# Loading the small state-space matrices of a hybrid decoder layer: C as four 128-row blocks, B with its states on the partitions

## The chip, the cores and the metric

The kernel runs on one core of one Trainium2 chip. The metric is the time of one execution on the device in microseconds; the runs of a kernel are summed up by their median. One execution was also recorded by the hardware profiler, and every time of an instruction below comes from that record. Its engines are PE (matrix multiply, with PEld for its weight loads), DVE (vector), ACT (activation), POOL and SP. Here SP does nothing but issue DMA transfers.

## The reference, cut to what matters

A layer on a sequence of 1,024 positions with 1,024 features: RMS norm, one input projection, two mixers (a diagonal complex state-space mixer and a short gated convolution), a gate for each, one output projection, a residual and a last norm. The change concerns the parameters of the state-space mixer, whose 32 groups have 16 channels (h) and 64 complex states (p) each:

```python
u32 = u.astype(f32).reshape(bsz, seq, SSM_N_GROUPS, SSM_GROUP)       # 32 groups x 16
q_re = (p_re * a_re + p_im * a_im) / den
q_im = (p_im * a_re - p_re * a_im) / den
bb_re = q_re[..., None] * b_re - q_im[..., None] * b_im              # b: (32 g, 64 p, 16 h)
bb_im = q_re[..., None] * b_im + q_im[..., None] * b_re
bu_re = jnp.einsum('blgh,gph->blgp', u32, bb_re)
bu_im = jnp.einsum('blgh,gph->blgp', u32, bb_im)
...
_, _, s_re, s_im = lax.associative_scan(
    _scan_combine, (a_seq_re, a_seq_im, bu_re, bu_im), axis=1)
y = (jnp.einsum('blgp,ghp->blgh', s_re, c_re.astype(f32))            # c: (32 g, 16 h, 64 p)
     - jnp.einsum('blgp,ghp->blgh', s_im, c_im.astype(f32))
     + d_skip.astype(f32) * u32)
```

In DRAM, c lies with p innermost (64 floats, 256 bytes in a row) and b with h innermost (16 floats, 64 bytes in a row).

## The kernel before

**Staging.** Products are float32 split into a high and a low part, so each is three matrix products ("h", "l", "x": weights high times input high, weights low times input high, weights high times input low). The input is 128 positions to a tile, eight tiles x0 to x7; they are normed on DVE, turned by PE transposes (`turn`), and written by ACT as xh (`gain`, L218) and by DVE as the low rest xl (`rest`, L224). The first projection computes u for four blocks of 128 channels (uw0 to uw3) and two halves of the positions. Then come the convolution's projections (`conv_hc`, `conv_bz`), among which the state-space mixer's steps for four blocks of eight groups are laid, then the gates and the output projection.

**The order at the start is written by hand.** The string START (L33 to L35) is run through token by token under a manual schedule for PE, ACT and DVE; each engine keeps this order. A letter names a step and digits its tiles: s = square of an x tile on ACT, n = norm on DVE, t = transposes of a pair of x tiles on PE, g = `gain` of that pair on ACT, x = `rest` on DVE, u/U = matrix products of u, k = `keep_u`, p = `transpose_params`, C = turned copies of C (L433 to L435), d = the next steps of `discretise` on DVE. The stretch that matters reads `k00 p0 u11lx. k10 t2 u21lx. k20 u31lx. k30 d12 g2 s6 x2 s7 C n67`. Behind the manual part a scheduler merges the rest of the program into each engine's order, by its own estimates.

**keep_u** (L241) copies a finished half block of u from PSUM to the SBUF tile `us` on ACT (L243), and SP stores it to the DRAM scratch `uscr` in four transfers of 64 KB (L245). The tile has two buffers, so the third copy (k20) needs the first's four stores to have landed, and the fourth (k30) the second's.

**The transfers** of all inputs are issued by SP in program order: x0, weights, x1 to x3, the small parameters, x4 to x7, and behind these the two loads of C into `craw` (32 groups on the partitions) and three loads of B into the rows 32 to 63 of `cb` (b_re, b_im, b_re), each of 32 rows of 4 KB. Completion of SP's transfers is told by eight semaphores used in turn; each transfer waits for the one eight places earlier.

**From C and B to c1, c2, b1, b2.** These four tiles [128, 32 groups, 16 h] hold the states of the real part on partitions 0 to 63 and of the imaginary part on 64 to 127 (c1 is (re, -im), c2 is (-im, -re), b1 is (re, im), b2 is (-im, re)). ACT first copies C with its axes turned into rows 0 to 31 of `cb`, three times (re, im, re; L435). `transpose_params(1)` and `(2)` (L270 to L277) then transpose, for each h, the 64 rows (32 groups of C, 32 of B) with 128 columns: 16 transposes each, 32 in all, in PSUM tiles of eight; ACT evicts each tile in two pieces, one to b and one to c, with the sign as a scale. b1 and b2 are read by the six `discretise` steps that make bb and bs (L396 to L401); c1 and c2 and these by `ssm_prep` (rr, vv; L499 to L505), whose result `vv` goes into the matrix products `ps_k` (L544).

Of the kernel before, what the change touches and what calls it, by code (L numbers as in the profile page):

```python
# [10 lines left out]
F32 = mybir.dt.float32  # L11
F32R = mybir.dt.float32r
I32 = mybir.dt.int32
AF = mybir.ActivationFunctionType
# [5 lines left out]
P = 128  # L20
# [3 lines left out]
C = L // T  # L24
KT = D // P
NB = 4
G = 8
NG = 32
H = 16
S = 64  # L30
EPS = 1e-6
WARM = (26, 8, 14)
START = ("s0 w0 n0 c s1 W0 n1 W1 w1 t0 L0 g0 L1 U010hl x0 u010x. W2 s2 s3 W3 L2 n23 u20hx u30hx t1 L3 g1 u230l. s4 x1 s5 n45 "  # L33
         "U01231h u01lx. k00 p0 u11lx. k10 t2 u21lx. k20 u31lx. k30 d12 g2 s6 x2 s7 C n67 d12 U01232h u01232l t3 g3 d8 x3 u01232x. "
         "U01233h u03l p1 p2 u03x. k01 u13lx. k11 d u23lx. k21 u33lx. k31")  # L35
ORDER = "p0 0 1 2 m0 q0 i0 3 p1 4 o0 5 6 m1 q1 i1 7 p2 8 o1 9 m2 q2 i2 10 p3 11 o2 m3 q3 i3 12 13 o3 14 15"
MAGIC = 12582912.0
# [20 lines left out]
def hybrid_kernel(ctx: ExitStack, tc, x, norm_gain, w_in, a_re, a_im, log_dt, b_re, b_im,  # L58
                  c_re, c_im, d_skip, w_glu, b_glu, conv_w, w_out, final_gain, out):
    nc = tc.nc  # L60
    V, A, Q, PE = nc.vector, nc.scalar, nc.gpsimd, nc.tensor

    const = ctx.enter_context(tc.tile_pool(name="const", bufs=1))
    big = ctx.enter_context(tc.tile_pool(name="big", bufs=1))
# [3 lines left out]
    psm = ctx.enter_context(tc.tile_pool(name="psm", bufs=4, space=PSUM))  # L68
# [6 lines left out]
    ident = const.tile([P, P], F32, name="ident")  # L75
    make_identity(nc, ident)
    sgn = const.tile([P, 1], F32, name="sgn")
    V.memset(sgn[0:S], 1.0)
    V.memset(sgn[S:P], -1.0)
    nsgn = const.tile([P, 1], F32, name="nsgn")  # L80
# [44 lines left out]
    pst = tc.alloc_tile_pool(name="pstage", bufs=1, side="right")  # L125
# [1 line left out]
    par = tc.alloc_tile_pool(name="par", bufs=1)  # L127
    xpool = tc.alloc_tile_pool(name="xstage", bufs=8)

    cb = big.tile([2 * NG, 3 * S * H], F32, tag="cy", name="cb")  # L130
    cb = cb.rearrange("g (r p h) -> g r p h", h=H, r=3)
    craw = pst.tile([NG, 2, H, S], F32, name="craw")
    lam_r = pst.tile([NG, 2, 2, S], F32, name="lam_r")
    ldt = pst.tile([P, NG], F32, name="ldt")
    d_r = pst.tile([NG, H], F32, name="d_r")
# [17 lines left out]
    def load(seq):  # L153
        for i in seq:
            if i == "w":
                n = len(raw)
                wr = (wst.tile([P, KT, P], F32, tag="wr", name=f"wru{n}", bufs=2) if n < 2 else
                      ysb[:, 1 if n == 2 else 3].rearrange("p (k n) -> p k n", k=KT))
                nc.sync.dma_start(wr, w_in_k[:, :, n * P:n * P + P])
                raw.append(wr)  # L160
            else:
                load_x(i)
# [7 lines left out]
    nc.sync.dma_start(rows, conv_w[0].rearrange("k (b p) -> (k b) p", p=P))  # L170
    nc.sync.dma_start(rowb, b_glu[0].rearrange("(b p) -> b p", p=P))
    load((4, 5, 6, 7))
    nc.sync.dma_start(craw[:, 0], c_re[0])
    nc.sync.dma_start(craw[:, 1], c_im[0])
    for k, src in enumerate((b_re, b_im, b_re)):
        nc.sync.dma_start(cb[NG:2 * NG, k], src[0])


    pw = pmm.tile([P, P], F32, tag="mm", name="ps_warm")
    def warm(count):  # L180
        for n in range(count):
            PE.transpose(pw, ident, ident)
# [4 lines left out]
    def square(i):  # L187
        ss = const.tile([P, 2], F32, tag="ss", name=f"ss{i}", bufs=4)
        sq = ysb[:, 2]
        sums[i] = []  # L190
        for k, c in enumerate(halves(i)):
            A.activation(sq[:, c], x_t[i][:, c], AF.Square, accum_out=ss[:, k:k + 1])
            sums[i].append(ss[:, k:k + 1])

    def norm(*tiles):
        todo = [rsqrt_steps(sums[i]) for i in tiles]
        for ops in itertools.zip_longest(*[ops for ops, _ in todo]):
            for op in filter(None, ops):
                op()
        for i, (_, r) in zip(tiles, todo):  # L200
            cut = D // 2 if i < 4 else D
            for c in range(0, D, cut):
                V.tensor_scalar_mul(x_t[i][:, c:c + cut], x_t[i][:, c:c + cut], r)
# [10 lines left out]
    def gain(pair, pss):  # L214
        n = slice(pair % 2 * 256, pair % 2 * 256 + 256)
        for kt in range(KT):
            ps = pss[kt // 2][:, kt % 2].rearrange("p a b -> p (a b)")
            A.activation(xh[pair // 2][:, kt, n], ps, AF.Copy, scale=g1[:, kt:kt + 1])  # L218
# [30 lines left out]
    lam = par.tile([P, 2, NG], F32, name="lam")  # L249
    c1 = par.tile([P, NG, H], F32, name="c1")  # L250
    c2 = par.tile([P, NG, H], F32, name="c2")
    b1 = pst.tile([P, NG, H], F32, name="b1")
    b2 = pst.tile([P, NG, H], F32, name="b2")
    dT = par.tile([H, NG], F32, name="dT")

    def transpose_params(part):
        if part == 0:
            ps = psm.tile([P, 2, NG], F32, tag="sm", name="ps_lam")
            for k in range(2):
                PE.transpose(ps[:, k], lam_r[:, k].rearrange("g d p -> g (d p)"), ident[0:NG, 0:NG])  # L260
            A.copy(lam, ps)
            ps = psm.tile([P, 16 + NG], F32, tag="sm", name="ps_rows")
            PE.transpose(ps[:, 0:12], rows, ident[0:12, 0:12])
            PE.transpose(ps[:, 12:16], rowb, ident[0:NB, 0:NB])
            PE.transpose(ps[0:H, 16:16 + NG], d_r, ident[0:NG, 0:NG])
            A.copy(cw, ps[:, 0:12])
            A.copy(bg, ps[:, 12:16])
            A.copy(dT, ps[0:H, 16:16 + NG])
            return
        off = part - 1  # L270
        for q in range(2):
            hs = slice(q * 8, q * 8 + 8)
            ps = psm.tile([P, 8, 2 * NG], F32, tag="sm", name=f"ps_cb{off}{q}")
            for h in range(8):
                PE.transpose(ps[:, h], cb[:, off:off + 2, :, 8 * q + h].rearrange("g r p -> g (r p)"), ident[0:2 * NG, 0:2 * NG])
            for dst, lo, scale in ((b2 if off else b1, NG, nsgn if off else 1.0), (c2 if off else c1, 0, -1.0 if off else sgn)):
                A.activation(dst[:, :, hs], ps[:, :, lo:lo + NG].rearrange("p h g -> p g h"), AF.Copy, scale=scale)  # L277

# [5 lines left out]
    def discretise(count=None):  # L286
        for op, args, kw in steps[:count]:
            op(*args, **kw)
        del steps[:count]
# [134 lines left out]
    with tc.manual_schedule(engines={mybir.EngineType.PE, mybir.EngineType.Activation, mybir.EngineType.DVE}):  # L424
        for what in START.split():
            n = [int(v) for v in what[1:] if v.isdigit()]
            if what[0] == "s":
                square(n[0])
            elif what[0] == "w":
                warm(WARM[n[0]])  # L430
            elif what[0] == "d":
                discretise(int(what[1:]) if what[1:] else None)
            elif what[0] == "C":  # L433
                for k in range(3):
                    A.copy(cb[0:NG, k], craw[:, k % 2].rearrange("g h p -> g p h"))  # L435
            elif what[0] == "c":
                ps = pmm.tile([P, KT], F32, tag="mm", name="ps_g1")
                PE.transpose(ps, g1r, ident[0:KT, 0:KT])
                V.tensor_copy(g1, ps)
            elif what[0] == "W":  # L440
                uw[n[0]] = [wst.tile([P, KT, P], F32R, tag=m, name=f"{m}u{n[0]}", bufs=4) for m in ("wh", "wl")]
                A.copy(uw[n[0]][0], raw[n[0]])
            elif what[0] == "L":
                V.tensor_tensor(uw[n[0]][1], raw[n[0]], uw[n[0]][0].bitcast(F32), SUB)
            elif what[0] == "n":
                norm(*n)
            elif what[0] == "t":
                turned[n[0]] = turn(n[0])
            elif what[0] == "g":
                gain(n[0], turned[n[0]])  # L450
            elif what[0] == "x":
                rest(n[0], turned[n[0]])
            elif what[0] == "p":
                transpose_params(n[0])
            elif what[0] in "uU":
                blocks, quarter = n[:-1], n[-1]
                cols = slice(quarter % 2 * 256, quarter % 2 * 256 + 256)
                parts = what.strip("uU0123.")
                for b in blocks:
                    if quarter % 2 == 0 and "h" in parts:  # L460
                        ups[b] = pmm.tile([P, 512], F32, tag="mm", name=f"mm_u{b}{quarter // 2}")
                if what[0] == "u":
                    todo = [(b, part, range(KT)) for b in blocks for part in parts]
                else:
                    todo = [(b, part, [kt - lag]) for kt in range(KT + 4) for lag, part in zip((0, 4), parts)
                            if 0 <= kt - lag < KT for b in blocks]
                for b, part, kts in todo:
                    product(uw[b], quarter // 2, ups[b], part, cols, what[-1] == "." and part == parts[-1], kts)
            else:
                keep_u(n[0], n[1], ups[n[0]])  # L470
# [7 lines left out]
    cy = big.tile([P, NB, L], F32, tag="cy", name="cy")  # L478
# [368 lines left out]
    for j in pairs:  # L847
# [32 lines left out]
        steps, r = rsqrt_steps([part[:, 2:3], part[:, 3:4], part[:, 4:5]])  # L880
# [44 lines left out]
```

## Time and profile before

| what | us |
|---|---|
| median of 3 runs | 437.37 |
| lowest and highest of them | 437.13, 706.63 |
| the profiled execution | 435.54 |
| its span, first to last instruction | 433.7 |
| PE busy in the span | 418.2 |
| DVE busy | 331.2 |
| ACT busy | 181.6 |

The profile's rows give the start and the duration in us, the engine, the line of the program, the operation, output and inputs by their names (numbers of buffers left out), the shape and the count of instructions merged into the row; in brackets stands how long the engine had been idle before it, and which instruction ended that. Rows of narrow stretches of time give busy shares of PE, PEld, DVE, ACT and POOL, the granted clock of PE, the busy share of the 16 DMA engines, and GB/s. DMA rows of a stretch count packets, which are the contiguous pieces of a transfer (with a few 4-byte ones that report completion).

### The profile page before, as it was taken

To read this page: it belongs to the slowest core of one execution; us is meant where nothing else is said; L and a number is where in the kernel's file an instruction comes from. 1 tells how busy PE (TensorE), PEld (TensorE's weight loads), DVE (VectorE), ACT (ScalarE), POOL (GpSimd) and SP (SyncE) were. 2 spreads that over 40 slices of the span, in tenths; PEclk is the share of its full clock that TensorE was granted. 3 is DMA by queue.
4 is the path that set the end of the run, shared out by engine and by line. 5 is a ranking of instruction groups with operands and counts; after the bars stand their busy time and mean duration, and the time that the engine had idled before them with its cause. 6 is when DMAs were issued, how large, how long until landed. Compare 5 with 4: busy or idle time off the path is not lost. (4 is left out here: it accounts for less than half of the span.)

```text
span 433.7 us, 6302 instructions
## 1 busy us (share of the span) xinstructions
PE 418.2 (96%) x2226; PEld 358.1 (83%) x2226; DVE 331.2 (76%) x821; ACT 181.6 (42%) x322; POOL 32.0 (7%) x39
## 2 busy tenths in 40 slices
PE   8998999999997999999999999999999999999991
PEld 8898999888887888888888888888888888888881
DVE  4973888969989979986996928746456799977734
ACT  4754933074213245135324414647434654333121
POOL 0000003001020020100021000211202100000011
PEclk9999999999999999999999999999999999999997
DMA  7983005433260641254025422577534540333212
GB/s 240 251 256 80 19 2 158 134 91 105 54 166 3 175 116 47 77 147 146 6 47 147 117 81 75 180 200 237 122 109 74 143 123 2 117 125 103 92 48 99
DMA packets 49472, 48.97 MB, mean 113 GB/s; under 512 B 6696, under 2 KB 39488, under 8 KB 49440
## 3 DMA queue, kind: packets, MB, share of 16 engines
q1 hardware_dynamic: 47568, 45.16, 35.5%
q0 software_dynamic: 1728, 3.15, 4.2%
q8 instruction: 17, 0.28, 0.3%
q10 hardware_dynamic: 144, 0.26, 0.2%
q14 instruction: 15, 0.12, 0.1%
HBM read 31.65 MB, written 8.39 MB: 92 GB/s over the span
## 5 line engine op out<-in xcount | busy, mean ns | idle before, releaser
L826 ACT ACTIVATE sq<-xr 128x512 f32<-128x512 f32 (+1 forms) x17 | 10.3, 606 | 41.8 <-DVE xr L823 30.1
L641 POOL TENSOR_TENSOR cy<-cy,sg 128x512 f32<-128x512 f32 x8 | 13.8, 1725 | 187.8 <-DVE sg L640 154.9
L747 PE MATMUL glu<-shl,wg 128*128 128x512 f32 x96 | 21.9, 389 | 0.0
L747 PEld LDWEIGHTS glu<-shl,wg 128*128 128x128 f32 x96 | 18.0, 188 | 3.7
L224 DVE SCALAR_TENSOR_TENSOR xl<-ps_x,g,xh 128x256 fp32r<-128x256 f32 x32 | 12.9, 474 | 8.6 <-ACT xh L218 8.6
L230 PE MATMUL mm_u<-xh,whu 128*128 128x256 f32 x128 | 17.5, 288 | 1.7 <-ACT xh L218 1.7
L230 PEld LDWEIGHTS mm_u<-xh,whu 128*128 128x128 f32 x128 | 16.2, 191 | 2.4 <-ACT xh L218 2.1
L230 PE MATMUL mm_u<-xh,wlu 128*128 128x256 f32 x128 | 17.9, 285 | 0.0
L230 PE MATMUL mm_u<-xl,whu 128*128 128x256 f32 x128 | 17.5, 284 | 0.0
L819 PE MATMUL ow<-bs,ax 128*128 128x512 f32 (+1 forms) x54 | 16.9, 367 | 0.5 <-DVE xr L823 0.5
L230 PE MATMUL mm_h<-xh,wlh 128*128 128x512 f32 x64 | 16.5, 394 | 0.0
L230 PE MATMUL mm_b<-xh,whb 128*128 128x512 f32 x64 | 16.5, 397 | 0.0
L230 PEld LDWEIGHTS mm_u<-xh,wlu 128*128 128x128 f32 x128 | 16.3, 191 | 0.1
L230 PEld LDWEIGHTS mm_u<-xl,whu 128*128 128x128 f32 x128 | 16.2, 192 | 0.1
L230 PE MATMUL mm_h<-xh,whh 128*128 128x512 f32 x64 | 16.1, 391 | 0.0
L230 PE MATMUL mm_b<-xl,whb 128*128 128x512 f32 x64 | 15.9, 390 | 0.0
L230 PE MATMUL mm_h<-xl,whh 128*128 128x512 f32 x64 | 15.8, 389 | 0.0
L230 PE MATMUL mm_c<-xh,whc 128*128 128x512 f32 x64 | 15.8, 389 | 0.0
L230 PE MATMUL mm_z<-xh,wlz 128*128 128x512 f32 x64 | 15.8, 389 | 0.0
L230 PE MATMUL mm_c<-xl,whc 128*128 128x512 f32 x64 | 15.8, 389 | 0.0
L230 PE MATMUL mm_z<-xl,whz 128*128 128x512 f32 x64 | 15.8, 389 | 0.0
L230 PE MATMUL mm_zs<-xh,wlzs 128*128 128x512 f32 x64 | 15.8, 389 | 0.0
(351 smaller groups left out, 1108.3 us busy)
## 6 DMA issues: line engine op xcount, KB each, us to landing
ee<-ec SPq DMA_DIRECT2D x16, 256.0 KB
wro<-in_w_out_dram SPq DMA_DIRECT2D x8, 512.0 KB
xr<-in_x_dram SPq DMA_DIRECT2D x8, 512.0 KB
out_dram<-xr SPq DMA_DIRECT2D x7, 512.0 KB
x<-in_x_dram SPq DMA_DIRECT2D x6, 512.0 KB
wrh<-in_w_in_dram SPq DMA_DIRECT2D x4, 512.0 KB
wrc<-in_w_in_dram SPq DMA_DIRECT2D x4, 512.0 KB
uscr<-us SPq DMA_DIRECT2D x32, 64.0 KB
```

The lines of the kernel that those rows point to most:

```text
L224: V.scalar_tensor_tensor(xl[pair // 2][:, kt, n], ps, g1[:, kt:kt + 1], hs.bitcast(F32), MUL, SUB)
L230: PE.matmul(ps[:, n], a[:, kt], b[half][:, kt, n], start=what == "h" and kt == 0, stop=last and kt == KT - 1)
L641: Q.tensor_tensor(yb[:, n], yb[:, n], sg, MUL)
L747: PE.matmul(ps, wg[:, a, k, es], shl[half][:, y, k], start=m + k == 0, stop=m == 2 and k == NB - 1)
L819: PE.matmul(out_, aq[op_a, j][:, p, k], bq[op_b, k][:, q, cols], start=first and m + k == 0, stop=m == 2 and k == NB - 1, skip_group_check ...
L826: A.activation(temp(f"sq{final_square.n}")[:, 0:x.shape[-1]], x, AF.Square, accum_out=acc)
```

## The change

C is loaded with 128 rows (8 groups by 16 h) on the partitions, for four blocks, with re, im and re beside one another (`craw`, [128, 4, 3, 64]). One transpose of 128x128 then gives one block of c1 (re, im) or of c2 (im, re), so that there are 2 x 4 transposes, each set of four in one PSUM tile and with one eviction. B is not transposed: SP loads b1 and b2 straight into their places, states on the partitions, by four transfers of 64 partitions x 32 groups x 16 floats, that is in pieces of 64 bytes at a distance of 4 KB in DRAM. b2's sign is set by one ACT operation in place. The token C goes, and the tile `cb` with it.

```diff
-         "U01231h u01lx. k00 p0 u11lx. k10 t2 u21lx. k20 u31lx. k30 d12 g2 s6 x2 s7 C n67 d12 U01232h u01232l t3 g3 d8 x3 u01232x. "
+         "U01231h u01lx. k00 p0 u11lx. k10 t2 u21lx. k20 u31lx. k30 d12 g2 s6 x2 s7 n67 d12 U01232h u01232l t3 g3 d8 x3 u01232x. "
...
-    cb = big.tile([2 * NG, 3 * S * H], F32, tag="cy", name="cb")
-    cb = cb.rearrange("g (r p h) -> g r p h", h=H, r=3)
-    craw = pst.tile([NG, 2, H, S], F32, name="craw")
+    craw = pst.tile([P, NB, 3, S], F32, name="craw")
...
-    nc.sync.dma_start(craw[:, 0], c_re[0])
-    nc.sync.dma_start(craw[:, 1], c_im[0])
-    for k, src in enumerate((b_re, b_im, b_re)):
-        nc.sync.dma_start(cb[NG:2 * NG, k], src[0])
+    for k, src in enumerate((c_re, c_im, c_re)):
+        nc.sync.dma_start(craw[:, :, k], src[0].rearrange("(b g) h p -> (g h) b p", g=G))
+    b1 = pst.tile([P, NG, H], F32, name="b1")
+    b2 = pst.tile([P, NG, H], F32, name="b2")
+    for dst, srcs in ((b1, (b_re, b_im)), (b2, (b_im, b_re))):
+        for k, src in enumerate(srcs):
+            nc.sync.dma_start(dst[k * S:k * S + S], src[0].rearrange("g p h -> p g h"))
...
-        for q in range(2):
-            hs = slice(q * 8, q * 8 + 8)
-            ps = psm.tile([P, 8, 2 * NG], F32, tag="sm", name=f"ps_cb{off}{q}")
-            for h in range(8):
-                PE.transpose(ps[:, h], cb[:, off:off + 2, :, 8 * q + h].rearrange("g r p -> g (r p)"), ident[0:2 * NG, 0:2 * NG])
-            for dst, lo, scale in ((b2 if off else b1, NG, nsgn if off else 1.0), (c2 if off else c1, 0, -1.0 if off else sgn)):
-                A.activation(dst[:, :, hs], ps[:, :, lo:lo + NG].rearrange("p h g -> p g h"), AF.Copy, scale=scale)
+        ps = psm.tile([P, NB, P], F32, tag="sm", name=f"ps_c{off}")
+        for b in range(NB):
+            PE.transpose(ps[:, b], craw[:, b, off:off + 2].rearrange("q r p -> q (r p)"), ident)
+        dst, scale = ((c1, sgn), (c2, -1.0))[off]
+        A.activation(dst.rearrange("p (b g) h -> p b (g h)", b=NB), ps, AF.Copy, scale=scale)
+        if off:
+            A.activation(b2, b2, AF.Copy, scale=nsgn)
...
-            elif what[0] == "C":
-                for k in range(3):
-                    A.copy(cb[0:NG, k], craw[:, k % 2].rearrange("g h p -> g p h"))
```

On SP, behind the last x tile, five loads of B and C stand before the first stores of u (us00 is the copy of step k00, us10 of k10; the semaphore that a transfer waits for is in brackets, DMAHW0 to DMAHW7 being the eight of SP's transfers). Before:

```order
L148 DMA x7_119<-in_x_dram 128x1024 [waits DMAHW0_49]
L173 DMA craw_104<-in_ssm_c_re_dram 32x1024 [waits DMAHW1_49]
L174 DMA craw_104<-in_ssm_c_im_dram 32x1024 [waits DMAHW2_49]
L176 DMA cb_103<-in_ssm_b_re_dram 32x1024 [waits DMAHW3_49]
L176 DMA cb_103<-in_ssm_b_im_dram 32x1024 [waits DMAHW4_49]
L176 DMA cb_103<-in_ssm_b_re_dram 32x1024 [waits DMAHW5_49]
L245 DMA uscr_151<-us00_563 8x16x128 [waits DMAHW6_49,Activation_49]
```

And now, to the stores of us10:

```order
L172 DMA craw_103<-in_ssm_c_re_dram 128x4x64 [waits DMAHW3_49]
L177 DMA b1_147<-in_ssm_b_re_dram 64x32x16 [waits DMAHW4_49]
L177 DMA b1_147<-in_ssm_b_im_dram 64x32x16 [waits DMAHW5_49]
L177 DMA b2_148<-in_ssm_b_im_dram 64x32x16 [waits DMAHW6_49]
L177 DMA b2_148<-in_ssm_b_re_dram 64x32x16 [waits DMAHW7_49]
L246 DMA uscr_154<-us00_564 8x16x128 [waits DMAHW0_49,Activation_49]
...
L246 DMA uscr_154<-us10_597 8x16x128 [waits DMAHW4_49,Activation_49]
L246 DMA uscr_154<-us10_597 8x16x128 [waits DMAHW5_49]
L246 DMA uscr_154<-us10_597 8x16x128 [waits DMAHW6_49]
L246 DMA uscr_154<-us10_597 8x16x128 [waits DMAHW7_49]
```

The four stores of us10 used to wait for C's and B's short loads; they now wait, one by one, for the four loads of B.

On ACT, at the third and fourth copy of u and at g2 behind them, the order is the same as before; this is how it reads now (ps_x20 to ps_x23 are the transposes of step t2, xh1 is xh of the second half):

```order
L244 COPY us10_597<-mm_u10_307 128x512 [waits PE_49]
L244 COPY us20_639<-mm_u20_401 128x512 [waits DMAHW1_49,DMAHW2_49,DMAHW0_49,DMAHW3_49,PE_49,Activation_49]
L244 COPY us30_661<-mm_u30_418 128x512 [waits DMAHW5_49,DMAHW6_49,DMAHW4_49,DMAHW7_49,PE_49,Activation_49]
L219 ACTIVATE xh1_85<-ps_x20_603,g1_110 128x256 x2
L219 ACTIVATE xh1_85<-ps_x21_604,g1_110 128x256 x2
L219 ACTIVATE xh1_85<-ps_x22_605,g1_110 128x256 x2
```

The copies of us20 and us30 wait for the four stores of us00 and of us10.

Further on ACT, where the scheduler places the last `discretise` copies (rotc) among the casts of the convolution's weights (whh1 and whc1 are those of its second block), before:

```order
L616 COPY hs00_1287<-mm_h00_1262 128x512
L288 ACTIVATE rotc_181<-rot_180 64x28x4 x3
L105 CAST whh1_1619<-wrh1_1617 128x1024
L288 ACTIVATE rotc_181<-rot_180 64x28x4 x3
L243 COPY us21_1163<-mm_u21_739 128x512
L243 COPY us31_1185<-mm_u31_740 128x512
L616 COPY hs01_1340<-mm_h01_1315 128x512
L105 CAST whc1_1625<-wrc1_1623 128x1024
```

And now:

```order
L612 COPY hs00_1254<-mm_h00_1229 128x512
L105 CAST whh1_1586<-wrh1_1584 128x1024
L287 ACTIVATE rotc_182<-rot_181 64x28x4 x6
L244 COPY us21_1130<-mm_u21_737 128x512
L244 COPY us31_1152<-mm_u31_738 128x512
L612 COPY hs01_1307<-mm_h01_1282 128x512
L105 CAST whc1_1592<-wrc1_1590 128x1024
```

The cast of whh1 has moved ahead of all six rotc copies.

More of the change, by code (lines that the diff above doesn't have):

```diff
@@ L251, in hybrid_kernel @@
     c2 = par.tile([P, NG, H], F32, name="c2")
-    b1 = pst.tile([P, NG, H], F32, name="b1")
-    b2 = pst.tile([P, NG, H], F32, name="b2")
     dT = par.tile([H, NG], F32, name="dT")
```

## The prediction

> **What bounds the kernel now.** I read the page first, then the waits of PE, then the timelines of PE, ACT and SP around the change, then the DMA rate in steps of 1 us, and last two short stretches in which one kind of DMA piece runs alone.
>
> The page's first part, and the list of who PE waited for in the whole span (us in total, times, longest):
>
> ```profile
> PE 418.2 (96%) x2226; PEld 358.1 (83%) x2226; DVE 331.2 (76%) x821; ACT 181.6 (42%) x322; POOL 32.0 (7%) x39
> PE ps_y L594 <- DVE ysb L583: 2.2, 1, 2.2
> PE mm_u L230 <- ACT xh L218: 1.7, 2, 1.1
> PE ow L819 <- DVE xr L823: 0.5, 1, 0.5
> PE ps_k L544 <- DVE vv L505: 0.2, 1, 0.2
> ```
>
> PE is the bound: it is busy 418.2 of 433.7 us, and these four waits add up to 4.6 us. So PE work taken away shortens the kernel only as far as the next wait does not grow, and whatever makes PE stand still lengthens it one for one. The change touches the first 65 us; this is PE there (start, us, operation, count):
>
> ```profile
> 41.24 4.10 PE L230 MATMUL mm_u<-xh,whu 128*128 128x256 f32 x32 [1.10 <-ACT xh L218]
> ...
> 49.01 1.91 PE L211 MATMUL ps_x<-ident,x 128*128 128x128 f32 x16
> 50.68 4.08 PE L230 MATMUL mm_u<-xl,whu 128*128 128x256 f32 x32
> ...
> 59.48 3.73 PE L275 MATMUL ps_cb<-ident,cb 64*128 64x64 f32 x32
> 63.15 1.21 PE L230 MATMUL mm_u<-xl,whu 128*128 128x256 f32 x8
> ```
>
> PE runs without a gap but for 1.10 us at 41.24, where it waits for the first xh of the second half (step g2), which ACT writes.
>
> **What is removed on PE.** The 32 transposes take 63.15 - 59.48 = 3.67 us of PE. A 128x128 transpose takes (50.68 - 49.01) / 16 = 0.104 us by the rows at 49.01 and 50.68, so the eight new ones take 0.84 us: 2.83 us less. Not all of it reaches the end. PE next meets DVE at ps_k:
>
> ```profile
> 89.42 1.23 DVE L106 TENSOR_TENSOR wlh<-wrh,whh 128x1024 fp32r<-128x1024 f32 x1 [1.84 <-ACT whh L105]
> 102.42 1.35 DVE L505 TENSOR_TENSOR vv<-vv,tv 128x1152 f32<-128x1152 f32 x1
> 103.83 1.27 PE L544 MATMUL ps_k<-vv,bb 128*16 128x128 f32 x10 [0.17 <-DVE vv L505]
> ```
>
> DVE ends vv at 103.77 and PE already waits 0.17 us for it. No DVE instruction is removed, so a PE that comes 2.83 us sooner mostly waits longer here. What can bring DVE forward is its 1.84 us of idling before wlh, since the order now puts the cast of whh ahead of all rotc copies on ACT. The gain that is left lies between 0 and 2.83 us; I take 1.0, nearer to the lower end, because the cast of whc that DVE needs next still stands behind those copies.
>
> **What is removed and added on ACT.** The rows of ACT (the eight evictions of L277 are shown by the first and the last):
>
> ```profile
> 38.30 0.59 ACT L243 COPY us<-mm_u 128x512 f32<-128x512 f32 x1 [3.12 <-PE mm_u L230]
> 40.22 0.59 ACT L243 COPY us<-mm_u 128x512 f32<-128x512 f32 x1 [1.33 <-PE mm_u L230]
> 40.70 3.04 ACT L218 ACTIVATE xh<-ps_x,g 128x256 fp32r<-128x256 f32 x8
> ...
> 45.86 5.94 ACT L435 COPY cb<-craw 32x1024 f32<-32x1024 f32 x3
> 51.71 2.96 ACT L218 ACTIVATE xh<-ps_x,g 128x256 fp32r<-128x256 f32 x8
> 60.61 0.38 ACT L277 ACTIVATE b<-ps_cb 128x256 f32<-128x256 f32 x1 [5.94 <-PE ps_cb L275]
> ...
> 63.63 0.38 ACT L277 ACTIVATE c<-ps_cb 128x256 f32<-128x256 f32 x1
> ```
>
> The three turned copies of C (5.94 us) go, and eight evictions of about 0.43 us (60.61 to 64.01, 3.40 us) become three operations of 128x512, which I price by the 128x512 copy of L243: 3 x 0.59 = 1.8 us. All of this I cost at nothing: ACT stood idle 5.94 us before the evictions. The copies pushed g3 (51.71) about 1 us behind its transposes, but PE wants g3's result only after the 32 matmuls that start at 50.68, that is at 54.59. If that cover were gone, at most that 1 us would show.
>
> **What is added on the DMA queue.** All loads go out on SP in one order. Rows of the issues (start, us), then the DMA rate in steps of 1 us (last number, GB/s) and three rows of narrower stretches:
>
> ```profile
> 21.24 1.21 SPq L173 DMA_DIRECT2D craw<-in_ssm_c_re_dram  x1
> ...
> 25.13 0.31 SPq L176 DMA_DIRECT2D cb<-in_ssm_b_re_dram  x1
> 32.72 7.39 SPq L245 DMA_DIRECT2D uscr<-us  x10
> 37.26 0.57 SPq L245 DMA_DIRECT2D uscr<-us  x1
> 27.00:28.00 1.00, 1.00 (x11) 1.00 (x10) 1.00 (x4) 0.97 (x3) 0.00 (x0) 1.00 1.13 352
> 28.00:29.00 1.00, 1.00 (x10) 1.00 (x10) 0.04 (x1) 1.00 (x2) 0.00 (x0) 1.00 1.08 209
> 29.00:30.00 1.00, 1.00 (x11) 1.00 (x10) 0.94 (x9) 0.03 (x1) 0.00 (x0) 1.00 1.05 156
> 30.00:31.00 1.00, 1.00 (x11) 1.00 (x10) 1.00 (x8) 0.00 (x0) 0.00 (x0) 1.00 0.69 131
> 31.00:32.00 1.00, 1.00 (x9) 0.87 (x8) 1.00 (x2) 0.00 (x0) 0.00 (x0) 1.00 0.41 90
> 32.00:33.00 1.00, 1.00 (x11) 0.94 (x11) 0.86 (x6) 0.87 (x5) 0.00 (x0) 1.00 0.04 16
> 38.00:39.00 1.00, 1.00 (x10) 1.00 (x10) 0.00 (x0) 0.59 (x1) 0.00 (x0) 1.00 0.42 111
> 39.00:40.00 1.00, 1.00 (x10) 0.94 (x8) 0.00 (x0) 0.00 (x0) 0.00 (x0) 1.00 0.03 9
> DMA packets 162, 0.01 MB, mean 48 GB/s; under 512 B 162, under 2 KB 162, under 8 KB 162
> ...
> q1 hardware_dynamic: 162, 0.01, 43.8%
> ...
> DMA packets 1175, 0.59 MB, mean 297 GB/s; under 512 B 16, under 2 KB 1175, under 8 KB 1175
> DMA packets 692, 0.15 MB, mean 75 GB/s; under 512 B 671, under 2 KB 671, under 8 KB 692
> ```
>
> The five loads of B and C hold 5 x 131,072 = 655,000 bytes, and after 28.0 the rates add up to 602,000. So they began at about 27.9, when the x loads ahead of them were through, though they were issued from 21.24: a later transfer of the queue moves behind the earlier ones. Then comes us, the copy of the projection that goes to DRAM.
>
> Now C is 3 x 512 pieces of 256 bytes and B is 4 x 2,048 pieces of 64 bytes, in place of 160 rows of 4 KB. Over 16 DMA engines that is 96 + 512 = 608 pieces each. The price of a piece comes from the last rows. They are the stretch 129.18 to 129.40, where the 64-byte pieces of a tp copy run (162 packets in 0.22 us on 16 engines, one per 21.7 ns on each); 13 to 15, 512-byte pieces of w_in out of DRAM (1,175 in 2 us, 27.2 ns); and 128 to 130, small pieces with gaps (692 in 2 us, 46.2 ns). I take 27.2, the row that also reads DRAM, for both sizes, and keep 21.7 and 46.2 as ends. B then ends at 27.9 + 608 x 0.0272 = 44.4 us (41.1 to 56.0), against 32.7 now.
>
> Two instructions wait for that. The tile us has two buffers, so ACT's third copy (38.30) waits until the first buffer's four stores have landed, and the fourth (40.22) until the second's have. Both sets stand behind B in the queue, and SP lets the second set go only as the four B loads complete. The last of these eight stores is issued at 37.26 now and the traffic is over at about 39.1 (9 GB/s in the step from 39), which is 1.8 us after the issue; with a little for the report of the landing I take 2.2. The fourth copy then starts at 44.4 + 2.2 = 46.6, not 40.22: 6.4 us late. In formula, the stall is 0.608 x (ns per piece) - 10.1 us, and it begins at 16.6 ns. Behind that copy on ACT stand g2 and the squares of x6 and x7, so PE waits for xh at 41.24, and DVE, which follows g2 in order, shifts too. The seven SP issues in place of five (0.3 to 1.2 us each) cost nothing: SP has no issue between 25.4 and 32.72.
>
> **The clock after the stall.** The warming transposes at the start:
>
> ```profile
> 1.37 5.81 PE L182 MATMUL ps_warm<-ident 128*128 128x128 f32 x26 [1.37 <-POOL ident masks.py:199]
> 9.16 1.69 PE L182 MATMUL ps_warm<-ident 128*128 128x128 f32 x14
> ```
>
> The first 26 take 0.223 us each, the later 14 0.121: a PE that has stood still runs at about half speed for up to 5.8 us, which loses up to 2.9 us. After the 1.10 us pause at 41.24 nothing of the kind shows (32 matmuls in 4.10 us, as in the block after). For a pause of 7.5 us I take 1.5, the middle of 0 and 2.9. The Trainium skill (TensorE: Matmul & The Clock Gate, Part 1) says that PE falls to half its clock after an idle window of about 3.4 us; by that rule the loss is an estimated 1.7 us and the sum 444.5.
>
> **The sum.** 6.4 + 1.5 - 1.0 = +6.9 us. The profiled execution's time is 435.54 (its span 433.7), so it would become 442.4; the median of the runs, 437.37, lies 1.8 above, and I state the prediction on that: 444.3 us.
>
> **The rivals.** (1) No stall. If a 64-byte piece costs less than 16.6 ns, B is through in time and only PE's gain stays: 436.4 (434.5 to 437.4). For it: in the tp stretch the packets' own time fills 43.8% of the engines, so one piece keeps an engine busy for only 9.5 ns. Against it: even there pieces follow each other at 21.7 ns. The Trainium skill (DMA: Bandwidth & Descriptors, Why small descriptors are slow) counts the bytes in beats of 32 plus about 3 cycles a packet; by that, 64 bytes take 5 cycles where 512 take 19, an estimated 7 ns here, and the time would be 436.4. The tp row disagrees with it so far.
>
> (2) Slow pieces, the end on the other side. Reading 64 bytes every 4 KB out of DRAM has no row here; at 46.2 ns the stall is 18.0 and the time 437.4 + 18.0 + 1.5 - 1.0 = 455.9. From 30.1 ns on (a stall of 8.2) the kernel is over 2% slower. For it: the price of my forecast is only 10% below that point.
>
> (3) PE gains its 2.83 us in full because DVE catches up during the stall. It can't be seen apart from the others by the time (442.5 with my stall), and DVE has nothing in its order that it could do before g2's result comes.
>
> **How the numbers follow.** My forecast (20 to 35 ns a piece) 0.5, rival 1 0.2, rival 2 0.3; the third lies inside the first. Leaving out the fastest part of rival 1 and the slowest of rival 2 gives 435 to 456; the forecast's own range is 440 to 449. About 2% (8.7 us) is what a measurement of this kernel can tell from no change: slower by more has rival 2 and the upper part of my forecast, 0.4; faster by more has 0.01, since 2.83 us is all there is to win; the rest, 0.59, lies within.
>
> **What would show it.** Right: DMA busy with small packets from about 28 to 44; the fourth us copy on ACT late by 6 us and released by the uscr stores; PE's longest wait at g2; the matmuls right after it slow; ps_k waiting longer for vv than 0.17. Wrong: small packets gone by 38, or PE at 41.24 still waiting only 1.1 us.

## The result, and the profile after

| | before | changed |
|---|---|---|
| median of 11 runs each, us | 436.64 | 434.67 |
| span of the profiled execution, us | 433.7 | 431.3 |
| PE busy, us | 418.2 | 414.9 |
| ACT busy, us | 181.6 | 174.2 |

The ratio of the times is 0.9949, with a 95% interval of 0.993 to 0.9968: half a per cent faster, about 2.2 us, which by the bound of 2% counts as no change. The forecast of 444.3 was wrong; 434.67 lies just below its range of 435 to 456, and near the 436.4 of the first rival (no stall). Of the difference to the forecast, 0.73 us is only the base: the forecast started from a median before of 437.37 (three runs), which is 436.64 over eleven.

The first page of the changed kernel, and the list of who PE waited for (us in total, times, longest):

```profile
PE 414.9 (96%) x2202; PEld 354.7 (82%) x2202; DVE 331.0 (77%) x821; ACT 174.2 (40%) x314; POOL 33.0 (8%) x39
...
PE mm_u L231 <- ACT xh L219: 2.5, 2, 1.8
PE ps_y L590 <- DVE ysb L579: 2.2, 1, 2.2
...
PE ps_k L540 <- DVE vv L501: 0.8, 1, 0.8
PE ow L815 <- DVE xr L819: 0.5, 1, 0.5
```

PE has lost 24 instructions and 3.3 us. Two waits grew: the one for xh (g2), 1.7 to 2.5 us in all, and the one at ps_k, 0.2 to 0.8. The timeline of the changed kernel shows these places, PE first, then SP, ACT and DVE (start, us, engine, operation, count, idle before):

```profile
41.55 4.09 PE L231 MATMUL mm_u<-xh,whu 128*128 128x256 f32 x32 [1.79 <-ACT xh L219]
...
59.70 1.04 PE L272 MATMUL ps_c<-ident,craw 128*128 128x128 f32 x8
60.50 1.19 PE L231 MATMUL mm_u<-xl,whu 128*128 128x256 f32 x8
...
102.00 1.27 PE L540 MATMUL ps_k<-vv,bb 128*16 128x128 f32 x10 [0.79 <-DVE vv L501]
...
24.42 0.74 SPq L177 DMA_DIRECT2D b<-in_ssm_b_re_dram  x1
25.20 6.68 SPq L177 DMA_DIRECT2D b<-in_ssm_b_im_dram  x2
31.93 1.30 SPq L177 DMA_DIRECT2D b<-in_ssm_b_re_dram  x1
33.33 10.50 SPq L246 DMA_DIRECT2D uscr<-us  x16
...
38.07 0.59 ACT L244 COPY us<-mm_u 128x512 f32<-128x512 f32 x1 [3.26 <-DMA uscr<-us]
40.54 0.59 ACT L244 COPY us<-mm_u 128x512 f32<-128x512 f32 x1 [1.89 <-DMA uscr<-us]
...
82.02 1.06 ACT L105 CAST whh<-wrh 128x1024 fp32r<-128x1024 f32 x1 [7.90 <-PE mm_h L231]
86.66 1.83 ACT L287 ACTIVATE rotc<-rot 64x112 f32<-64x112 f32 x6 [3.58 <-DVE rot L287]
...
86.64 1.23 DVE L106 TENSOR_TENSOR wlh<-wrh,whh 128x1024 fp32r<-128x1024 f32 x1
100.59 1.35 DVE L501 TENSOR_TENSOR vv<-vv,tv 128x1152 f32<-128x1152 f32 x1
```

The reader is to see four things. The eight transposes take 60.50 - 59.70 = 0.80 us where the 32 took 3.67. The third and fourth copies of u are now released by the stores (uscr), as forecast, but the fourth starts at 40.54 and not at 46.6; PE waits 1.79 us at g2 instead of 1.10, and its 32 products then take 4.09 us (before: 4.10), so the clock is not lowered. SP spends 24.42 to 33.23 issuing the four loads of B, and its first store of u leaves at 33.33 (before: 32.72). And DVE ends vv at 101.94 instead of 103.77, since ACT casts whh at 82.02, long before DVE wants it.

How long PE takes from its first product of u to ps_k shows the sum without the start, which varies by up to 1.1 us between executions. Before it was 103.83 - 12.30 = 91.53 us; now it is 102.00 - 11.93 = 90.07. Of the 2.87 us saved on transposes, 0.69 went to the longer wait at g2 and 0.62 to the longer wait at ps_k, which leaves 1.56 (measured: 1.46). From ps_k to PE's last product both take 320.4 us. The rest of the difference of the spans, 0.9 us, is 0.37 at the start and the remainder behind PE's last product; one execution of each doesn't tell whether the change has a part in it.

The DMA counts of the stretch from 28 to 36.5, and three steps of 1 us in it (the last two numbers are the DMA engines' busy share and GB/s):

```profile
DMA packets 8897, 0.77 MB, mean 90 GB/s; under 512 B 8614, under 2 KB 8896, under 8 KB 8896
...
31.00:32.00 1.00, 1.00 (x11) 0.83 (x10) 0.97 (x4) 0.27 (x1) 0.00 (x0) 1.00 0.38 33
32.00:33.00 1.00, 1.00 (x10) 0.99 (x9) 0.83 (x6) 0.61 (x5) 0.00 (x0) 1.00 0.29 29
...
36.00:37.00 1.00, 1.00 (x11) 1.00 (x10) 0.00 (x0) 0.00 (x0) 0.00 (x0) 1.00 0.41 111
```

With 16 engines, 8,897 packets in 8.5 us are one per 15.3 ns on each, and that holds two slack microseconds (31 to 33). From 36 on the rate is that of the stores of u (111 GB/s, as before): the small pieces are through about 8 us sooner than the forecast's 44.4.

### The profile page after: what moved, and what is told of

The parts are those of the page before. It is cut to its first block, busy times and chain, and to the rows that moved or that the text cites. A ratio compares the mean times of both kernels' runs of the same rounds, so it can differ in the third digit from the quotient of the medians.

```text
span 431.3 us, 6243 instructions
## 1 busy us (share of the span) xinstructions
PE 414.9 (96%) x2202; PEld 354.7 (82%) x2202; DVE 331.0 (77%) x821; ACT 174.2 (40%) x314; POOL 33.0 (8%) x39
## 5 line engine op out<-in xcount | busy, mean ns | idle before, releaser
L231 PE MATMUL mm_b<-xh,whb 128*128 128x512 f32 x64 | 16.6, 399 | 0.0
```

The source lines that it names most:

```text
L231: PE.matmul(ps[:, n], a[:, kt], b[half][:, kt, n], start=what == "h" and kt == 0, stop=last and kt == KT - 1)
```

## The experiments

The theory after the result: a small piece costs well under the 16.6 ns from which the stall grows, PE's saved transposes are the whole gain, and the longer g2 wait is the price of the little that B's loads delay the stores. Its rivals: the pieces are slow and something else hid them; the gain is ACT's, not PE's; B's loads still cost something that can be had back. All ratios below are to the kernel before, run on the same chip; the other numbers are of one profiled execution each.

| kernel | ratio, 95% interval | wait at g2 | 32 products after it | transposes | first u product to ps_k |
|---|---|---|---|---|---|
| before | 1 | 1.10 | 4.10 | 3.67 | 91.53 |
| changed | 0.9949 (0.993, 0.9968) | 1.79 | 4.09 | 0.80 | 90.07 |
| changed, again | 0.9946 (0.9925, 0.9966) | 2.66 | 6.75 | 0.80 | 92.52 |
| B twice | 1.0159 (1.0126, 1.0193) | 7.71 | 5.97 | 0.80 | 98.44 |
| B late | 0.9963 (0.9943, 0.9982) | 1.09 | 4.10 | 0.80 | 89.50 |
| B as rows | 0.9914 (0.989, 0.9938) | 1.09 | 4.10 | 0.80 | 89.43 |
| half of B | 0.9957 (0.9937, 0.9977) | 1.09 | 4.10 | 0.80 | 90.21 |
| four buffers | 0.9922 (0.9901, 0.9944) | 1.05 | 4.09 | 0.80 | 89.26 |
| four buffers, again | 0.9943 (0.9924, 0.9962) | 1.05 | 4.09 | 0.80 | 89.39 |
| transposes back | 0.9994 (0.9973, 1.0014) | 2.13 | 4.09 | 2.70 | 91.57 |
| ACT copies back | 0.9962 (0.9937, 0.9986) | 2.04 | 4.09 | 0.80 | 90.22 |
| C alone | 1.0032 (1.0013, 1.0051) | 1.09 | 4.10 | 4.87 | 92.58 |
| B alone | 1.0032 (0.9999, 1.0065) | 2.83 | 5.58 | 3.71 | 95.97 |

### What a small piece costs

**B twice.** A second set of B's loads, never read, stands behind the first:

```diff
+    b1x = pst.tile([P, NG, H], F32, name="b1x")
+    b2x = pst.tile([P, NG, H], F32, name="b2x")
+    for dst, srcs in ((b1x, (b_re, b_im)), (b2x, (b_im, b_re))):
+        for k, src in enumerate(srcs):
+            nc.sync.dma_start(dst[k * S:k * S + S], src[0].rearrange("g p h -> p g h"))
```

> The changed kernel with the four B loads made twice (the second set into two tiles that nothing reads), ahead of the stores of u. Theory 1 (14.6 ns per 64-byte piece on each engine, from 28.9 to 36.4 for 512 pieces, stall one for one): B ends 7.5 us later, the fourth copy of u starts at about 48 and PE's wait at g2 is about 9.3 us; with the clock unhurt the time is 7.5 us above the changed kernel (442), with PE at half speed for some us after the pause (a matmul block at g2 of 5.5 us or more instead of 4.1) it is 1.4 to 3 more. Rival (the stores of u are not held behind B, the 0.7 us are only SP's issue): about 1 us above the changed kernel.

It came out at 443.47 us, 1.6% slower. DMA counts of its stretch from 34 to 41, its timeline of SP, ACT and PE, and a stretch of 3 us (the number before the last two is the granted clock):

```profile
DMA packets 9791, 0.62 MB, mean 89 GB/s; under 512 B 9791, under 2 KB 9791, under 8 KB 9791
...
q1 hardware_dynamic: 9791, 0.62, 92.8%
...
33.98 1.66 SPq L182 DMA_DIRECT2D b1x<-in_ssm_b_re_dram  x1
...
38.41 1.60 SPq L182 DMA_DIRECT2D b2x<-in_ssm_b_re_dram  x1
40.11 10.42 SPq L251 DMA_DIRECT2D uscr<-us  x16
...
44.80 0.58 ACT L249 COPY us<-mm_u 128x512 f32<-128x512 f32 x1 [9.15 <-DMA uscr<-us]
47.30 0.58 ACT L249 COPY us<-mm_u 128x512 f32<-128x512 f32 x1 [1.91 <-DMA uscr<-us]
...
48.31 5.97 PE L236 MATMUL mm_u<-xh,whu 128*128 128x256 f32 x32 [7.71 <-ACT xh L224]
...
48.00:51.00 3.00, 2.69 (x12) 2.69 (x13) 2.35 (x6) 3.00 (x9) 0.00 (x0) 0.50 0.40 107
```

This stretch is 7 us of almost nothing but 64-byte pieces, with the engines 92.8% busy: 16 x 7 / 9,791 = 11.4 ns a piece on each engine. What it does to the kernel looks like the forecast: the copies of u late by 7 us, PE standing 7.71 us at g2, half a clock (0.50) behind it, and 5.97 - 4.10 = 1.87 us lost by it. But the path is another. The forecast let the stores wait in the DMA queue, behind B's pieces. Two numbers order the copies here: the third starts 4.7 us after SP's first store in both kernels (33.33 to 38.07, 40.11 to 44.80), and the fourth 2.5 us behind that. SP issues the eight stores one by one, about 0.62 us apart (the eighth at 38.21 in the changed kernel, whose landing lets the fourth copy go at 40.54). What delays the copies is therefore when SP comes to issue the first store, and it comes to it only when it has issued the last load of B: at 33.33 in the changed kernel, where the data of that store had been ready at 32.32.

**B as rows** takes the small pieces out: b1 and b2 get the same bytes in rows of 2 KB. It leaves out B's arrangement by states, so its b1 and b2 are other numbers.

```diff
-            nc.sync.dma_start(dst[k * S:k * S + S], src[0].rearrange("g p h -> p g h"))
+            nc.sync.dma_start(dst[k * S:k * S + S].rearrange("p g h -> p (g h)"), src[0].rearrange("g (t q) h -> (g t) (q h)", t=2))
```

> The changed kernel with B's loads as whole 2 KB rows, the same bytes in 64 rows each; leaves out B's arrangement by states, so the output is not the reference's. Theory 1 (the number of pieces is what delays): SP issues the stores at about 32.3, the fourth copy waits for PE, the span is about 430.6. Rival (bytes or transfers count, not pieces): the fourth copy is still late by 0.7 us.

**B late** issues the same loads of B only behind DVE's rest step x2, when the stores that the copies wait for are gone (they are taken out at the old place; the memset of one column on DVE makes each pair of loads wait for DVE):

```diff
+                if n[0] == 2:
+                    for dst, srcs in ((b1, (b_re, b_im)), (b2, (b_im, b_re))):
+                        V.memset(dst[:, 0, 0:1], 0.0)
+                        for k, src in enumerate(srcs):
+                            nc.sync.dma_start(dst[k * S:k * S + S], src[0].rearrange("g p h -> p g h"))
```

> The changed kernel with the four B loads issued only when DVE has finished the xl of step x2 (about 45 us), behind the first sixteen stores of u. Theory 1 (what is left of the stall is the 64-byte pieces and their issue ahead of the stores of u): ACT's third and fourth copy of u wait for PE again and not for the stores, PE's wait at g2 falls from 1.79 to about 1.1 us, and the span from 431.3 to about 430.6. Rival (the copies were late for another reason, C's 256-byte pieces): g2 stays late by 0.7 and the time stays that of the changed kernel.

SP's issues of B as rows:

```profile
26.13 0.59 SPq L177 DMA_DIRECT2D b<-in_ssm_b_re_dram  x1
26.76 1.22 SPq L177 DMA_DIRECT2D b<-in_ssm_b_im_dram  x2
28.26 0.47 SPq L177 DMA_DIRECT2D b<-in_ssm_b_re_dram  x1
33.28 11.16 SPq L246 DMA_DIRECT2D uscr<-us  x16
```

Both put the wait at g2 back to 1.09. As rows, B's loads hold SP for 2.6 us and the stores are again not held by them; as small pieces they hold it for 8.8 us in the changed kernel, and for 5.4 us as late loads (45.60 to 51.04), behind the stores. B as rows gives the lowest ratio of all, but from four executions, and its distance to the changed kernel (0.9949 to 0.9914, 1.5 us, with intervals that overlap) can't be read as the price of the small pieces. All four had a mean granted clock (the share of its full speed that PE was given) of 0.993 or 0.994; of the changed kernel's eleven, five had that, at 432.2 to 434.3 us, and six had 0.982 to 0.991, at 434.7 to 438.7 us. Among executions of 0.993 or more the four (433.1 to 433.5 us) are no faster. Late loads give no better time than the changed kernel either (eight of their twelve executions lie at 0.991 or less): the 0.7 us is too small to be told in the time.

Where the lower clock of such executions comes from can be seen in the profiles. Behind the wait for ysb at 137 to 146 us (ps_y, 1.95 to 2.42 us in all profiles) the granted clock stays 1.00 in some executions and is 0.50 for 3.4 us in others, of one and the same kernel too: both profiles of the changed kernel wait 2.18 us there, and only the second has the clock at 0.50, from 141.4 to 144.8. From ps_k to PE's last product it then takes 322.1 us instead of 320.4. The gain of the change does not rest on this: among executions of 0.992 or more on one chip, the kernel before has a mean of 435.70 us (8 of 28) and the changed kernel 434.11 (5 of 12), which is 1.6 us less.

**Half of B**: only b1 is loaded in small pieces, 4,096 of them, and ACT makes b2 from it across the halves.

```diff
+    for k, src in enumerate((b_re, b_im)):
+        nc.sync.dma_start(b1[k * S:k * S + S], src[0].rearrange("g p h -> p g h"))
...
-            A.activation(b2, b2, AF.Copy, scale=nsgn)
+            A.activation(b2[0:S], b1[S:P], AF.Copy, scale=-1.0)
+            A.copy(b2[S:P], b1[0:S])
```

> The changed kernel with b1 alone loaded (two transfers, 4,096 pieces of 64 bytes in place of 8,192); b2 is made from b1 by two ACT operations across the partition halves. Theory 1 (SP is held by the issue of the pieces, and every 2,048 pieces hold it some 1.4 us longer): SP's first store of u goes as soon as its data are there, the fourth copy of u waits for PE, PE's wait at g2 is about 1.1 us and the ratio to before about 0.992. Rival (one late transfer is enough to hold the stores): PE still waits 1.8 us, ratio 0.995.

The stores now leave on time (first at 32.76) and the wait at g2 is 1.09, but at 89.71 PE meets a new wait of 0.72 us for ACT's copy of u. The time is not better than that of the changed kernel (0.9957, where 0.992 was expected).

### Where the gain comes from

**Transposes back**: 24 transposes of the identity, 64x64, whose results nobody reads, follow the eight new ones.

```diff
+        pd = psm.tile([P, 8, 2 * NG], F32, tag="sm", name=f"ps_d{off}")
+        for n in range(12):
+            PE.transpose(pd[0:2 * NG, n % 8], ident[0:2 * NG, 0:2 * NG], ident[0:2 * NG, 0:2 * NG])
```

> The changed kernel with 24 transposes of 64x64 of the identity put back on PE beside the eight (12 in each of the two steps), which nothing reads; ACT and the loads stay as changed. Theory 1 (all of the gain comes from the 2.87 us of PE): the two steps take about 3.6 us of PE again and the time is at or a little above that of before (ratio 1.000, from 0.998 to 1.003, since the 0.7 us wait at g2 stays). Rival (the gain comes from the 5.9 us of copies that ACT lost, or from the order behind it): ratio 0.995 as in the changed kernel.

**ACT copies back**: three copies of 32x1,024, with turned axes, at the old place of C in ACT's order; they read x tiles and write a tile that nobody reads.

```diff
+            elif what[0] == "C":
+                dump = xw.tile([NG, H, S], F32, name="dump")
+                for k in range(3):
+                    A.copy(dump, x_t[k][0:NG].rearrange("g (p h) -> g p h", p=H))
```

> The changed kernel with three copies of 32x1024 (turned, out of the first x tiles into a tile that nothing reads) put back on ACT where the turned copies of C stood. Theory 1 (ACT's 5.9 us were beside other work): the time stays that of the changed kernel, ratio 0.995. Rival: the ratio goes back towards 1.000.

With the transposes back, the gain is gone (0.9994); with the copies back it stays (0.9962). The timeline of the first shows PE, ACT and DVE:

```profile
60.77 0.60 PE L272 MATMUL ps_c<-ident,craw 128*128 128x128 f32 x4
61.30 0.86 PE L275 MATMUL ps_d<-ident 64*64 64x64 f32 x12
62.09 0.66 PE L272 MATMUL ps_c<-ident,craw 128*128 128x128 f32 x4
62.68 0.86 PE L275 MATMUL ps_d<-ident 64*64 64x64 f32 x12
...
90.21 1.04 ACT L105 CAST whh<-wrh 128x1024 fp32r<-128x1024 f32 x1
...
91.28 1.22 DVE L106 TENSOR_TENSOR wlh<-wrh,whh 128x1024 fp32r<-128x1024 f32 x1 [2.45 <-ACT whh L105]
102.35 1.35 DVE L504 TENSOR_TENSOR vv<-vv,tv 128x1152 f32<-128x1152 f32 x1
```

The 32 transposes take 2.70 us here, 1.0 less than before, and the wait at g2 is 1.0 longer (2.13), so the two cancel. But the scheduler, which counts the 24 transposes too, has also put most of the rotc copies back ahead of the cast of whh, and DVE idles 2.45 us there again. So this kernel undoes two things at once: PE's time, and the early cast that lets DVE follow. Which part of the gain would survive with the transposes gone and the cast late was not tried. An estimate comes from DVE's end of vv, counted from PE's first product of u: 91.05 us here (12.65 to 103.70), 90.01 in the changed kernel (11.93 to 101.94). So with the cast late, about 1 of the 1.46 us would have been lost at ps_k again; the longer wait at g2 is a part of that, and DVE's order differs in other places too. The ACT copies took 3.19 us for three, not 5.94, so they bound the worth of ACT's saving only to that size; they stood behind g2 and in no one's way (ACT waited 1.25 us for PE after them, before g3).

**C alone** keeps the new C and transposes B from rows as before (16 transposes for b1 and 16 for b2, 32 rows each). **B alone** keeps the new B and transposes C from rows.

```diff
+        ps = psm.tile([P, H, NG], F32, tag="sm", name=f"ps_b{off}")
+        for h in range(H):
+            PE.transpose(ps[:, h], cb[:, off:off + 2, :, h].rearrange("g r p -> g (r p)"), ident[0:NG, 0:NG])
+        A.activation((b2 if off else b1), ps.rearrange("p h g -> p g h"), AF.Copy, scale=nsgn if off else 1.0)
```

> C as in the changed kernel, B as before (three loads of 32 rows of 4 KB, then 32 transposes of 32 rows and two evictions). Theory 1: no small pieces, so PE's wait at g2 is about 1.1 us; but PE has 32 + 8 transposes, about 4.5 us, 0.8 more than before, so the ratio is about 1.002. Rival (C's part carries the gain): 0.995.

```diff
-            PE.transpose(ps[:, b], craw[:, b, off:off + 2].rearrange("q r p -> q (r p)"), ident)
+        for h in range(H):
+            PE.transpose(ps[:, h], cb[:, off:off + 2, :, h].rearrange("g r p -> g (r p)"), ident[0:NG, 0:NG])
```

> B as in the changed kernel, C as before (two loads of 32 rows, three turned copies on ACT, 32 transposes of 32 rows). Theory 1: PE keeps 32 transposes (about 3.7 us) and has the longer wait at g2, up to 0.7 us more than 1.1, so the ratio is 1.000 to 1.002. Rival (B's part carries the gain, by ACT's fewer evictions): 0.995.

Neither half pays: both came out at 1.0032, B alone with an interval that just includes 1. The first reason is in the count of transposes. C alone has 8 + 32 of them (4.87 us), B alone 32 (3.71 us), since each of the old transposes turned C and B together. Only both halves at once take them away. PE in the timeline of C alone, and of B alone:

```profile
59.47 0.60 PE L274 MATMUL ps_c<-ident,craw 128*128 128x128 f32 x4
60.00 1.95 PE L279 MATMUL ps_b<-ident,cb 32*128 32x32 f32 x16
```

```profile
43.01 5.58 PE L232 MATMUL mm_u<-xh,whu 128*128 128x256 f32 x32 [2.83 <-ACT xh L220]
```

B alone pays, in this execution, for small pieces as well: 2.83 us of waiting at g2 and 5.58 - 4.10 = 1.48 us of lost clock. A second spell of half clock, from 67.3 to 70.7 us, is the rest of its 95.97. It came without a stop: PE was busy all the time from 46.9, at the end with the 32 transposes.

### Can the small loss be had back?

**Four buffers** for us, so that no copy of the first half waits for a store:

```diff
-        us = xw.tile([P, 4, C], F32, tag="us", name=f"us{b}{half}", bufs=2)
+        us = xw.tile([P, 4, C], F32, tag="us", name=f"us{b}{half}", bufs=4)
```

> The changed kernel with four buffers for the copies of u, so that no copy waits for a store; B is loaded where it was. Theory 1: the fourth copy starts as PE ends its block (about 39.9), PE's wait at g2 falls to about 1.1 us, the time is that of the kernel with B late (span about 430.6). Rival: the DMA traffic itself delays something else, then only B late is faster.

It gave 0.9922, and PE's wait at g2 was 1.05. To see whether it is really ahead of the changed kernel, both were run again, side by side.

> The kernel with four buffers for the copies of u once more, beside the changed kernel on one chip: 0.992, and 0.7 us below the changed kernel if the wait at g2 is all that is between them. Rival (the two are the same within the spread of runs): no difference.

> The changed kernel once more, for the comparison on one chip: ratio 0.995, PE's wait at g2 between 1.8 and 2.1 us.

They came out at 0.9943 and 0.9946: by time the two can't be told apart. That the first measurement had 0.9922 goes with the clock again: five of its six executions had 0.992 or more, three of eleven in the second. What differs is what single executions do. The changed kernel's second profile, the timeline of ACT and PE and two stretches of 5 us:

```profile
39.61 0.59 ACT L244 COPY us<-mm_u 128x512 f32<-128x512 f32 x1 [4.08 <-DMA uscr<-us]
...
43.15 6.75 PE L231 MATMUL mm_u<-xh,whu 128*128 128x256 f32 x32 [2.66 <-ACT xh L219]
...
40.00:45.00 5.00, 2.34 (x13) 2.14 (x12) 1.51 (x4) 3.06 (x9) 0.00 (x0) 0.74 0.39 106
45.00:50.00 5.00, 5.00 (x29) 5.00 (x28) 3.97 (x22) 2.83 (x6) 0.00 (x0) 0.58 0.14 37
```

Here the same kernel waits 2.66 us at g2 instead of 1.79, its clock falls to 0.58 in the step from 45, and the 32 products take 6.75 us: 2.65 us lost, on top of the wait. This execution took 438.01 us, the longest of its 12 (median 434.39). The stretch to ps_k is 92.52 us there, longer than before the change, against 89.26 and 89.39 with four buffers, where the wait stayed 1.05 in both profiles although SP's first store in the second left at 34.49. Four of the 23 executions of the changed kernel have a mean clock of 0.986 or less, as this one has (0.983), and none of the 17 with four buffers. That the stop at g2 is the cause in all four isn't shown: five of C alone's ten have it too, and PE waits only 1.09 us at g2 in that kernel's profile.

## Why the prediction was wrong

**The price of a piece was the failing step.** The prediction took 27.2 ns, with ends at 21.7 and 46.2; in a steady run it is 11.4, outside both. Both rows it stood on measured something else. The 512-byte row had the engines fully busy (a share of 1.17) at 297 GB/s, with eight times the bytes in a piece. Since a piece of 64 bytes takes 11.4 ns, most of the 27.2 went with the bytes and not with the piece. The tp row was 162 packets in 0.22 us, some ten for each engine, with the engines 43.8% busy, so for over half of the time they had no piece to move: presumably start and end of a short transfer. What the packets themselves kept an engine busy for there, 9.5 ns, was the better guide, and the text had it, as the argument of rival 1. The Trainium skill (DMA: Bandwidth & Descriptors, Why small descriptors are slow) had given an estimate of 7 ns a piece by its beats; 11.4 lies above it, but below the 16.6 from which the stall grows, so the conclusion drawn from that section held and mine did not.

**The formula for the stall left out SP.** By it, 11.4 ns gives 0.608 x 11.4 - 10.1 = -3.2 and 15.3 ns gives -0.8: no stall from the pieces' time, which is right. It does not give the time of the fourth copy, though. With twice B, 27.9 + 1,120 x 0.0114 + 2.2 makes 42.9 us, and the copy started at 47.30. The term that fails is one that was costed at nothing, "the seven SP issues in place of five". They were put at 0.3 to 1.2 us each; the four of B took 8.8 us together, the first store left 0.61 us late (1.0 us after its data were ready), and from it to the fourth copy there are 7.2 us in both kernels (33.33 to 40.54, 40.11 to 47.30). That is the whole of the measured delay of the fourth copy, 0.69 us against PE's own pace. What followed once the stall was there, with twice the loads, came on the instructions and with the clock loss that were forecast.

**PE's gain was mis-sized.** The removal was right (2.87 us, forecast 2.83; eight transposes 0.80, forecast 0.84). Of it 1.0 us was said to survive at ps_k; 2.25 did, since only 0.62 turned into waiting there. The prediction named the cause that brings DVE forward, the cast of whh ahead of the rotc copies, but took its effect for small because the cast of whc stayed behind. Yet that cast came sooner too. These are rows of ACT and DVE before, and then of after:

```profile
87.52 0.93 ACT L288 ACTIVATE rotc<-rot 64x112 f32<-64x112 f32 x3 [10.95 <-DVE rot L288]
88.35 1.03 ACT L105 CAST whh<-wrh 128x1024 fp32r<-128x1024 f32 x1
...
91.93 1.05 ACT L105 CAST whc<-wrc 128x1024 fp32r<-128x1024 f32 x1
...
93.02 1.23 DVE L106 TENSOR_TENSOR wlc<-wrc,whc 128x1024 fp32r<-128x1024 f32 x1 [2.37 <-ACT whc L105]
```

```profile
90.10 1.05 ACT L105 CAST whc<-wrc 128x1024 fp32r<-128x1024 f32 x1
...
91.19 1.23 DVE L106 TENSOR_TENSOR wlc<-wrc,whc 128x1024 fp32r<-128x1024 f32 x1 [3.32 <-ACT whc L105]
```

The rotc copies start 0.86 us sooner (87.52 to 86.66), and the cast of whh, 1.03 us, no longer stands among them: together 1.89, and whc comes 1.83 us sooner, as vv does. Of this, 0.37 is the earlier start of the execution; the other 1.46 is the gain. The prediction's reason was not wrong in kind: of the 1.84 us that DVE no longer idles before wlh, 0.95 came back as a longer wait for whc (2.37 to 3.32). With four buffers the stretch to ps_k shows what the change gives when g2 isn't late: 91.53 - 89.26 = 2.27 and 91.53 - 89.39 = 2.14 us.

**ACT's savings were worth nothing**, as said, as far as 3.19 us of copies put back can show. The three new operations took 0.69, 0.59 and 0.72 us and run from 60.34 to 62.13, 1.79 us for the forecast's 1.8.

**The clock** was right in kind: 1.87 us after a stop of 7.71, forecast 1.5 for 7.5, which was the middle of a range from 0 to 2.9. In the changed kernel such a stop didn't occur in either profile; the second lost 2.65 us behind a stop of 2.66.

**The chances.** Rival 1 had 0.2 and is what happened, with a stall of 0.69 us by SP instead of none. That 434.67 lies inside its 434.5 to 437.4 is in part luck, since the base was 0.73 too high. Rival 3 did not come: behind the 7.71 us stop of B twice, PE still waited 0.77 us for vv. That a kernel can't gain more than about 2.8 us here was right, and so was the small chance of faster by 2%.

## What to carry to other kernels

Price a small DMA piece from a long, steady run of such pieces, with their own busy time as the floor; a short transfer with engines half idle gives too high a price. Count the time for which the issuing engine is held by a transfer of thousands of pieces, because everything behind it in that order leaves later. When two versions differ by less than 1%, compare executions of the same granted clock: here a spell of half clock far behind the change made 1.7 us of difference, about as much as the change itself. Before a saving on the busiest engine is cut down to the next wait, follow the engine it will wait for: the same saving can bring that one forward, and half of such a change may be worth nothing without the other half.

## What the hardware showed that was not expected

SP is held by long lists of small pieces: 8.8 us for four transfers of 2,048 pieces in the changed kernel, of which the second and third took 6.68 us, where rows of 2 KB took 2.6 us. The length of the list alone doesn't set it. The first transfer held SP 0.74 us; the second, of the same length, held it 3.84 us behind the x loads, and 1.88 us in B late, where the x loads were long through. In the steady stretch of B twice it is 1.23 to 1.66 us a transfer, and 2,048 pieces on 16 engines at 11.4 ns take 1.46. That fits an SP that waits for room in the queue. But in 31 to 33, while SP was still issuing, the DMA engines were only 0.38 and 0.29 busy. Whether SP waits there for room or takes that long by itself stays open.

The granted clock fell to 0.50 after stops at g2 of 2.66 and 2.83 us (the 32 products took 6.75 and 5.58 us), and not after stops of 1.79, 2.04 and 2.13 us (4.09 us each). That is not a threshold: at ps_y it fell after stops of 2.12 (transposes back), 2.18 (changed, again), 2.20 (half of B) and 2.42 us (C alone), and not after 2.17 to 2.21 us in seven other profiles. The spells of half clock lasted 3.4 us or twice that. The Trainium skill (TensorE: Matmul & The Clock Gate, Part 1) puts the idle window at about 3.4 us; all of these stops, as the profile shows them, are shorter, and the measurement decides. What picks the executions that lose the clock stays open.

A transpose's price hardly depends on its rows. It goes with its weight load (PEld): 200 ns for 64 rows before and 198 ns for 32 rows in C alone, where the columns of `cb` that are read lie 16 floats apart, and 140 ns for 128 rows of the new `craw` and 134 ns for 32 rows of lam_r, which are read without gaps. So the old transposes took 0.117 us each and those of C alone 0.12, the new ones 0.10, and the 24 of the 64x64 identity about 0.07. That the distance in the reading is what costs fits these rows, but no run changes it alone.
